# A gated recurrence inside a decoder step: token pairs up to 32 apart as 32x32 products in one PSUM tile

## The chip, the cores and the metric

The program runs on 1 core of one Trainium2 chip. The time is device microseconds from launch to end, one number for each execution; smaller is better.

## What is computed

One inference step of a two-layer decoder, for a prompt of 1024 tokens and 8 single-token samples with a paged cache of 8192 tokens each. Each layer has an input projection, four groups of heads (sparse attention, the HGRN2 recurrence, pooling, memory attention) and an output projection. The change is in the recurrence of the prompt. The reference runs it in chunks of tokens; with G the running sum of the log gates inside a chunk, it computes

```python
diff = Gc[:, :, :, None, :] - Gc[:, :, None, :, :]
dec = jnp.exp(jnp.where(causal[None, None, :, :, None], diff, -jnp.inf))
A = jnp.einsum('bhtd,bhtsd->bhts', qc, dec * kc[:, :, None, :, :])
o = jnp.einsum('bhts,bhsv->bhtv', A, vc) + jnp.einsum('bhtd,bhdv->bhtv', qc * jnp.exp(Gc), S)
```

There are 4 heads of 64 channels. A[t, s] is a sum over channels of q[t] exp(G[t] - G[s]) k[s] for s <= t. The decay depends on the channel and on both tokens, so A is no plain product of two matrices.

## The kernel before

Each layer runs through four phases, A, P2, P3 and O. A scheduler places the instructions of a phase on each engine's own queue, by priority and by modelled times, so that one stretch of work fills the gaps of another. The change lies in P3. There two stretches share the engines. `stageC` compresses the whole cache of the 8 samples: it gathers cache rows into `R` (SyncE, ScalarE and GpSimd issue the transfers), copies a part of them on VectorE (line 544), turns them on TensorE into `ct` (line 246), splits `ct` into a high and a low half (`Xh` on ScalarE at line 564, `Xl` on VectorE at line 565), and multiplies them by `w1h` and `w1l` into `ch` (lines 120 to 122). Its 16 units per layer have the lower priority. The other stretch, with the higher priority, is the sample set-up, the recurrence (`hgrn`), and after it the window and memory attention of the samples.

`hgrn_pair` takes two heads at a time, 64 channels each, on the 128 partitions, and 1024 tokens in four pieces of 256. For each piece `hgrn_blocks` is called once: 8 calls a layer, 16 in the program. A call works on two blocks `j` of 128 tokens and two heads `e`. To get A by matrix products it uses levels lv = 64, 32, 16, 8, 4, 2, 1. At a level the block is cut into groups of 2 lv tokens, and `decayed(lv)` makes a tile `hKQ` (VectorE subtracts, ScalarE takes exponents into `hE`, GpSimd multiplies) that holds in the first half of each group k times its decay to the middle of the group, and in the second half q times its own. The product of first halves with second halves gives the pairs that first part company at this level. The diagonal is k times q (line 1410).

- Levels 64, 32 and 16: TensorE writes each group's square straight to its place in a PSUM tile `bv` (line 1417), on top of the diagonal product; VectorE masks `bv` into the SBUF tile `hAT` (line 1421).
- Levels 8, 4, 2 and 1: TensorE multiplies each whole block of 128 tokens by itself (line 1429), and VectorE copies the pairs that belong to the level into `hAT` under a mask (line 1432), once for each head and level.

Then TensorE multiplies `hAT` by the values (line 1440), beside the product of `qG` with the state (line 1438), into one PSUM tile `O`. A product of float32 operands is two passes of a weight load and a matmul each, and the trace counts passes. In P3 the recurrence's lane has two PSUM tiles of kind `mt` and one of kind `ma` (`psT` and `psA`).

Of the kernel before, what the change touches and what calls it, by code (L numbers as in the profile page):

```python
# [9 lines left out]
F32 = mybir.dt.float32  # L10
# [4 lines left out]
U8 = mybir.dt.uint8  # L15
# [19 lines left out]
LEVELS = (8, 4, 2, 1)  # L35
# [5 lines left out]
def _const_array():  # L41
# [15 lines left out]
    put("causT", (i[:, None] <= i[None, :]))  # L57
# [22 lines left out]
    for lv in LEVELS:  # L80
        same = (i[:, None] // (2 * lv)) == (i[None, :] // (2 * lv))
        put(f"lev{lv}", same & (i[:, None] % (2 * lv) < lv) & (i[None, :] % (2 * lv) >= lv))
# [30 lines left out]
class Net:  # L113
# [52 lines left out]
    def setup(self, ctx):  # L166
# [8 lines left out]
        self.lev = {lv: self.cp.tile([128, 128], U8, name=f"levm{lv}") for lv in LEVELS}  # L175
# [23 lines left out]
    def late_setup(self, tp):  # L199
# [5 lines left out]
        for lv in LEVELS:  # L205
            nc.vector.tensor_copy(self.lev[lv], self.cc(tp, f"lev{lv}"))
# [1008 lines left out]
    def hgrn(self, l, pp, wk, nb=1):  # L1215
# [6 lines left out]
        for x in self.hst:  # L1222
            nc.gpsimd.memset(x, 0.0)
# [124 lines left out]
    def hgrn_blocks(self, l, hp, b, t0_, q, k, G, G3, EGl, hv, S0, gB, wk):  # L1348
# [39 lines left out]
        def decayed(lv):  # L1388

            E = t1("hE", 4)  # L1390
# [14 lines left out]
        cT = self.c("causT").unsqueeze(1).to_broadcast([128, 2, 128])  # L1405
        bv = [self.psA()[:, :256].rearrange("p (j t) -> p j t", j=2) for _ in range(2)]
        for e, hs in enumerate(half):
            for j in range(2):
                t0 = (b + j) * 128
# [9 lines left out]
        AT = [wk.tile([128, 2, 128], F32, name="hAT") for _ in range(2)]  # L1419
        for e in range(2):  # L1420
            nc.vector.tensor_tensor(AT[e], bv[e], cT, op=OP.mult)
        for g in range(2):
            ps = [self.psT() for _ in range(2)]
            for m in range(2):
                x = decayed(LEVELS[g * 2 + m])
                for e, hs in enumerate(half):
                    for j in range(2):
                        xj = x[hs, j * 128:j * 128 + 128]
                        mm(ps[e][:, m * 256 + j * 128:m * 256 + j * 128 + 128], xj, xj, start=True, stop=True)  # L1429
            for e in range(2):  # L1430
                for m in range(2):
# [369 lines left out]
```

## Time and profile before

| | |
|---|---|
| time before, median of 3 runs | 2343.73 us (2340.57 to 2345.09) |
| profiled execution | 2343.6 us, its span 2341.8 us |
| TensorE busy, of the span | 87% |
| VectorE busy | 65% |
| ScalarE busy | 38% |
| GpSimd busy | 32% |
| mean granted TensorE clock | 0.93 |
| recurrence in layer 0 and layer 1 | about 609 to 868 us and 1757 to 2061 us |

The busy shares are over the whole span. What a change in the recurrence is worth is read from the two stretches in which it runs.

### The profile page before, as it was taken

Reading aid. Unit: us, or ns where it says so; the run is one execution under the profiler, and the core shown is the slowest. Engines: PE = TensorE matmul, PEld = TensorE weight load, DVE = VectorE, ACT = ScalarE, POOL = GpSimd, SP = SyncE. Lnnn points to the kernel's source line nnn. Section 1 sums busy time; section 2 is a strip of 40 time slices with the busy share of each in tenths; the row PEclk is TensorE's granted clock in tenths of the full one; section 3 lists DMA queues with packets and bytes.
Section 4 is the critical chain, followed back from the end, with each engine's and each line's share of the span. In section 5 each row is a group of like instructions: output and inputs, shape, how many; then the busy total and the mean of one; then the engine's idle time right before and its main releaser. Section 6 shows DMA issues by size and latency. Waiting matters only on the chain.

```text
span 2341.8 us, 41952 instructions
## 1 busy us (share of the span) xinstructions
PE 2048.5 (87%) x14396; PEld 1824.7 (78%) x14396; DVE 1511.6 (65%) x3927; ACT 888.2 (38%) x2221; POOL 746.7 (32%) x841
## 2 busy tenths in 40 slices
PE   4999998894798999896979999898949899998878
PEld 4997888784788888785669979887838888878645
DVE  7874377885777666553298724788867776656523
ACT  4223366553433323230152234675545333333101
POOL 2002123313655543223020012243146555532340
PEclk8999999997899899898989999999969998998889
DMA  7237321106655446776253363221086544467661
GB/s 249 92 109 184 94 78 52 58 26 169 176 146 149 119 125 184 201 235 200 87 171 105 112 155 98 66 61 47 28 208 170 140 135 136 138 190 221 174 206 51
DMA packets 324093, 312.97 MB, mean 134 GB/s; under 512 B 60619, under 2 KB 285783, under 8 KB 323608
## 3 DMA queue, kind: packets, MB, share of 16 engines
q1 hardware_dynamic: 261544, 213.25, 31.1%
q0 software_dynamic: 24320, 79.71, 11.7%
q10 hardware_dynamic: 38016, 17.32, 2.8%
q8 instruction: 115, 1.88, 0.3%
q14 instruction: 98, 0.80, 0.1%
HBM read 255.00 MB, written 59.57 MB: 134 GB/s over the span
## 4 chain that ended last, share of the span: by engine, by line
PE 58%; DVE 16%; DMA 11%; issue 8%; ACT 3%; POOL 2%; SPq 2%; ACTq 0%; DVEq 0%; another core or an unknown queue 0%; POOLq 0%
PE ch L120 3%; PE ch L122 3%; PE mt L246 3%; PE ct L246 3%; PE ch L121 3%; PE aa L121 3%; PE aa L122 3%; PE aa L120 3%; PE mt L1429 2%; PE oa L122 2%; PE oa L120 2%; PE oa L121 2%; DVE P L804 2%; PE fa L120 2%; PE fa L122 2%
## 5 line engine op out<-in xcount | busy, mean ns | idle before, releaser
L524 POOL DMA_INDIRECT R<-in_cache_nsa_dram,idxc x256 | 253.1, 989 | 295.8 <-PE ct L246 192.5
L120 PE MATMUL ch<-w1h,Xh 128*128 128x256 f32 x1024 | 314.3, 307 | 17.6 <-ACT Xh L564 8.7
L122 PE MATMUL ch<-w1h,Xl 128*128 128x256 f32 x1024 | 311.4, 304 | 6.1 <-DVE Xl L565 3.2
L121 PE MATMUL ch<-w1l,Xh 128*128 128x256 f32 x1024 | 308.7, 301 | 0.4 <-issue 0.4
L120 PEld LDWEIGHTS ch<-w1h,Xh 128*128 128x128 f32 x1024 | 209.1, 204 | 23.5 <-ACT Xh L564 10.2
L122 PEld LDWEIGHTS ch<-w1h,Xl 128*128 128x128 f32 x1024 | 208.4, 204 | 13.8 <-DVE Xl L565 5.7
L148 POOL TENSOR_TENSOR wl<-wf,wh 128x1024 fp32r<-128x1024 f32 (+2 forms) x42 | 94.9, 2271 | 377.1 <-ACT wh L139 295.6
L564 ACT CAST Xh<-ct 128x512 fp32r<-128x512 f32 x256 | 146.0, 585 | 180.0 <-PE ct L246 109.9
L121 PEld LDWEIGHTS ch<-w1l,Xh 128*128 128x128 f32 x1024 | 209.0, 204 | 2.0 <-issue 0.4
L565 DVE TENSOR_TENSOR Xl<-ct,Xh 128x512 fp32r<-128x512 f32 x256 | 172.4, 683 | 42.8 <-ACT Xh L564 26.1
L246 PE MATMUL ct<-cst,R 128*128 128x128 f32 x1024 | 163.9, 292 | 40.7 <-DVE Xl L565 31.0
L246 PEld LDWEIGHTS ct<-cst,R 128*128 128x128 f32 x1024 | 122.1, 149 | 53.2 <-DVE Xl L565 33.7
L544 DVE COPY R<-R 128x256 f32<-128x256 f32 x260 | 92.5, 370 | 107.5 <-DMA R<-in_cache_nsa_dram,idxc 68.9
L121 PE MATMUL aa<-wl,hTh 128*128 128x326 f32 (+1 forms) x512 | 156.6, 307 | 5.1 <-POOL wl L148 5.1
L120 PE MATMUL aa<-wh,hTh 128*128 128x326 f32 (+1 forms) x512 | 156.4, 307 | 4.0 <-ACT wh L139 4.0
L122 PE MATMUL aa<-wh,hTl 128*128 128x326 f32 (+1 forms) x512 | 156.1, 305 | 0.0
L447 ACT ACTIVATE P<-ms,nst 128x512 f32<-128x512 f32 (+3 forms) x192 | 106.6, 557 | 78.7 <-DVE nst L777 78.0
L120 PE MATMUL fa<-hTh,wh 128*128 128x344 f32 x384 | 129.4, 337 | 4.2 <-ACT fo L381 3.9
L122 PE MATMUL fa<-hTh,wl 128*128 128x344 f32 x384 | 125.1, 326 | 0.0
L121 PE MATMUL fa<-hTl,wh 128*128 128x344 f32 x384 | 125.1, 326 | 0.0
L820 DVE TENSOR_TENSOR pl<-mt,ph 128x512 fp32r<-128x512 f32 (+1 forms) x160 | 101.2, 644 | 33.9 <-ACT ph L819 29.0
L777 DVE TENSOR_REDUCE nst<-ms 128x1 f32<-128x512 f32 (+3 forms) x192 | 98.0, 517 | 32.4 <-PE ms L774 19.2
(558 smaller groups left out, 5722.9 us busy)
## 6 DMA issues: line engine op xcount, KB each, us to landing
wf<-in_w_in_dram SPq DMA_DIRECT2D x34, 512.0 KB
R<-in_cache_nsa_dram SPq DMA_DIRECT2D x256, 64.0 KB
R<-in_cache_nsa_dram ACTq DMA_DIRECT2D x256, 64.0 KB
zd<-fo SPq DMA_DIRECT2D x48, 172.0 KB
pwf<-in_cmp_w_dram SPq DMA_DIRECT2D x32, 256.0 KB
wof<-in_w_out_dram SPq DMA_DIRECT2D x16, 512.0 KB
oo<-od SPq DMA_DIRECT2D x16, 512.0 KB
oz<-zd SPq DMA_DIRECT2D x16, 512.0 KB
```

What stands on the lines that cost most here:

```text
L120: mm(out, lh, rh, start=first, stop=False)
L121: mm(out, lh, rl, start=False, stop=False)
L122: mm(out, ll, rh, start=False, stop=last)
L148: e.tensor_tensor(lo, src, hi.bitcast(F32), op=OP.subtract)
L246: self.nc.tensor.transpose(out, in_, self.ident[:in_.shape[0], :in_.shape[0]])
L447: self.nc.scalar.activation(out, S, AF.Exp, bias=nm, accum_out=sm)
L524: nc.gpsimd.indirect_dma_start(R[:, j].rearrange("p c d -> p (c d)"), None, rows, bass.IndirectOffsetOnAxis(ap=self.idxc[:, l, at + j:at + ...
L544: nc.vector.tensor_copy(Rs[:, :, :, 2], R[:, :, 0:2])
L564: nc.scalar.copy(hi, pv)
L565: nc.vector.tensor_tensor(lo, pv, hi.bitcast(F32), op=OP.subtract)
L777: nc.vector.tensor_reduce(one(nm), S, axis=AX.X, op=OP.max, negate=True)
L820: nc.vector.tensor_tensor(pl[:, :n], ps[:, :n], ph[:, :n].bitcast(F32), op=OP.subtract)
```

## The change

All levels up to 16 become products of 32 tokens by 32 tokens. For each head, one PSUM tile holds for both blocks six products (k by q, and levels 16, 8, 4, 2, 1), each in 32 columns: the four groups of 32 tokens in a block stand on the four quarters of the partitions. VectorE multiplies the whole 128x384 tile by one mask (`near`: the diagonal, and one pattern for each level) into `hpn` and sums the six products into `hC`, 128x64. Levels 64 and 32 go to a PSUM tile `far`, and ScalarE copies their three pieces into a tile `hA` which was zeroed once (four such tiles take turns). `O` is now the product of `hA` with the values, plus four 32-row products of `hC` with the values. `causT`, the four level masks and their set-up go; `hE` has 3 buffers and not 4.

```diff
-LEVELS = (8, 4, 2, 1)
+LEVELS = (16, 8, 4, 2, 1)
...
-        for x in self.hst:
+        self.hat = [pp.tile([128, 2, 128], F32, name=f"hA{n}") for n in range(4)]
+        for x in self.hst + self.hat:
             nc.gpsimd.memset(x, 0.0)
...
-            E = t1("hE", 4)
+            E = t1("hE", 3)
             x = t1("hKQ", 5)
...
-                mm(bv[e][:, j], k[hs, t0:t0 + 128], q[hs, t0:t0 + 128], start=True, stop=True)
-        for lv in (64, 32, 16):
-            x = decayed(lv)
-            for e, hs in enumerate(half):
+        x64, x32 = decayed(64), decayed(32)
+        xs = [(k[:, sl], q[:, sl])] + [(x, x) for x in map(decayed, LEVELS)]
+        near = self.c("near").rearrange("p (m t) -> p m t", t=32).unsqueeze(1)
+        for e, hs in enumerate(half):
+            far = self.psA()[:, :192].rearrange("p (j t) -> p j t", j=2)
+            for j in range(2):
+                a0 = j * 128
+                mm(far[:, j, 0:64], x64[hs, a0:a0 + 128], x64[hs, a0 + 64:a0 + 128], start=True, stop=True)
+                for p in (0, 64):
+                    mm(far[p:p + 64, j, 64:96], x32[hs, a0 + p:a0 + p + 64], x32[hs, a0 + p + 32:a0 + p + 64],
+                       start=True, stop=True)
+            nc.scalar.copy(A[0:64, :, 64:128], far[0:64, :, 0:64])
+            for p in (0, 64):
+                nc.scalar.copy(A[p:p + 32, :, p + 32:p + 64], far[p:p + 32, :, 64:96])
...
+            ps = self.psT()[:, :2 * m * 32].rearrange("p (j m t) -> p j m t", j=2, m=m)
+            for n, (xk, xq) in enumerate(xs):
                 for j in range(2):
-                    for p in range(0, 128, 2 * lv):
-                        a0 = j * 128 + p
-                        mm(bv[e][p:p + lv, j, p + lv:p + 2 * lv], x[hs, a0:a0 + lv], x[hs, a0 + lv:a0 + 2 * lv],
-                           start=True, stop=True)
-            nc.vector.tensor_tensor(AT[e], bv[e], cT, op=OP.mult)
...
-                        mm(ps[e][:, m * 256 + j * 128:m * 256 + j * 128 + 128], xj, xj, start=True, stop=True)
-                    nc.vector.copy_predicated(AT[e], self.lev[LEVELS[g * 2 + m]].unsqueeze(1).to_broadcast([128, 2, 128]),
-                                              ps[e][:, m * 256:m * 256 + 256].rearrange("p (j t) -> p j t", j=2))
+                    for p in range(0, 128, 32):
+                        a0 = slice(j * 128 + p, j * 128 + p + 32)
+                        mm(ps[p:p + 32, j, n], xk[hs, a0], xq[hs, a0], start=True, stop=True)
+            nc.vector.tensor_tensor(pn, ps, near.to_broadcast([128, 2, m, 32]), op=OP.mult)
+            nc.vector.tensor_reduce(c, pn.rearrange("p j m t -> p j t m"), axis=AX.X, op=OP.add)
...
-                mm(O[:, j, e], AT[e][:, j], hv[:, b + j, e * 64:e * 64 + 64], start=S[j] is None, stop=S[j] is None or e == 1)
+                mm(O[:, j, e], AT[e][:, j], v, start=S[j] is None, stop=False)
+                for p in range(0, 128, 32):
+                    mm(O[ps, j, e], C[e][ps, j], v[ps], start=False, stop=S[j] is None or e == 1, tile_position=(p, p))
```

The scheduler works the order out anew for phases P3 and O; A and P2 keep theirs but for the mask set-up. On TensorE, in the second call of layer 0, the queue before holds the diagonal and the direct squares of one head (1410, 1417), then whole-block products (1429), between the cache's transposes `ct`; sizes are weights by moving columns, and x counts products of two passes each:

```order
L1410 MATMUL ma<-hq,hk 128x128 x2
L1417 MATMUL ma<-hKQ 64x64 x2
L1417 MATMUL ma<-hKQ 32x32 x4
L1417 MATMUL ma<-hKQ 16x16 x8
L606 MATMUL ch<-w_8493,hh 128x128
L246 MATMUL ct<-cst,R_9073 128x128
L609 MATMUL ch<-w_8493,hl 128x64
L246 MATMUL mt<-cst,ot 128x128 x2
L1429 MATMUL mt<-hKQ 128x128 x4
```

In the changed kernel, whose line numbers are its own, the same call has the far products (1414, 1416), then nearly all 96 near products (1430) in one go, and later the output (1440, 1443, 1446):

```order
L1414 MATMUL ma<-hKQ 128x64
L1416 MATMUL ma<-hKQ 64x32 x2
L1414 MATMUL ma<-hKQ 128x64
L1416 MATMUL ma<-hKQ 64x32 x2
L243 MATMUL mt<-cst,ot 128x128 x2
L1430 MATMUL mt<-hq,hk 32x32 x8
L1430 MATMUL mt<-hKQ 32x32 x24
L1440 MATMUL ma<-hS_6592,hqG 128x128
L1443 MATMUL ma<-hv,hA_6599 128x64
L1430 MATMUL mt<-hKQ 32x32 x8
L1430 MATMUL mt<-hq,hk 32x32 x8
L1430 MATMUL mt<-hKQ 32x32 x48
```

The short products stand closer together than any before, and the large ones are gone. Over a layer the last product of the recurrence stands behind 799 of the layer's 1696 `ch` products, where it stood behind 1036; in layer 1 it stands 192 `ch` products earlier.

On VectorE, at the third call of layer 0 before, eight masked copies of the call (1432, masks `levm`) lie between the cache's `Xl` (565) and `R` (544):

```order
L1432 COPY_PREDICATED hAT<-levm_64,mt 128x256
L1432 COPY_PREDICATED hAT<-levm_65,mt 128x256
L586 TENSOR_TENSOR xs<-ch,cbias 128x256
L565 TENSOR_TENSOR Xl_9523<-ct,Xh_9522 128x16x32
L544 COPY R_9665<-R_9665 128x2x2x64
L565 TENSOR_TENSOR Xl_9521<-ct,Xh_9520 128x16x32
L1432 COPY_PREDICATED hAT<-levm_64,mt 128x256
L544 COPY R_9649<-R_9649 128x4x64
L588 SCALAR_TENSOR_TENSOR xs<-xth,xs 128x256
L1432 COPY_PREDICATED hAT<-levm_66,mt 128x256
```

After, a call has two pairs of a product (1432) and a sum (1434) there:

```order
L1432 TENSOR_TENSOR hpn<-mt,cst 128x384
L562 TENSOR_TENSOR Xl_10123<-ct,Xh_10122 128x16x32
L1434 TENSOR_REDUCE hC<-hpn 128x64
L617 TENSOR_TENSOR vo<-ch,vo 128x64
L562 TENSOR_TENSOR Xl_10121<-ct,Xh_10120 128x16x32
L541 COPY R_10245<-R_10245 128x2x2x64
L541 COPY R_10229<-R_10229 128x4x64
L1432 TENSOR_TENSOR hpn<-mt,cst 128x384
L1434 TENSOR_REDUCE hC<-hpn 128x64
```

Ten VectorE instructions of a call, two maskings and eight copies, have become four.

## Rows read from the trace of the kernel before

**Rows 1.** The page, busy us of each engine, share of the span, instructions.

```profile
PE 2048.5 (87%) x14396; PEld 1824.7 (78%) x14396; DVE 1511.6 (65%) x3927; ACT 888.2 (38%) x2221; POOL 746.7 (32%) x841
```

**Rows 2.** Busy time by stretch: start:end, length, five engines, clock, DMA share, GB/s.

```profile
609.00:868.00 259.00, 236.90 (x2166) 216.05 (x2164) 183.89 (x499) 94.63 (x284) 143.92 (x213) 0.93 0.49 137
868.00:1000.00 132.00, 119.77 (x916) 108.07 (x915) 77.21 (x198) 40.57 (x91) 46.44 (x49) 0.95 0.64 181
1000.00:1060.00 60.00, 57.69 (x318) 48.74 (x316) 34.03 (x65) 16.29 (x28) 7.85 (x11) 0.94 0.81 240
1757.00:2061.00 304.00, 284.47 (x2535) 261.56 (x2535) 213.66 (x579) 114.39 (x318) 166.44 (x240) 0.93 0.53 146
```

**Rows 3.** TensorE's waits, 609 to 868 us: total us, times, longest.

```profile
PE ct L246 <- DVE Xl L565: 7.1, 4, 3.6
PE ct L246 <- DVE hE L1396: 3.1, 1, 3.1
PE ma L1410 <- DVE hS L1384: 2.5, 2, 1.9
PE ch L122 <- DVE Xl L565: 2.2, 2, 1.6
```

**Rows 4.** TensorE in order of time, layer 1: start us, us, instruction, passes.

```profile
1971.89 0.41 PE L1417 MATMUL ma<-hKQ 64*32 64x32 f32 x24
1972.23 1.16 PE L1429 MATMUL mt<-hKQ 64*128 64x128 f32 x8
1973.32 1.10 PE L246 MATMUL ct<-cst,R 128*128 128x128 f32 x8
```

**Rows 5.** The same view: one head's direct products, and a run of two passes.

```profile
631.53 0.71 PE L1410 MATMUL ma<-hq,hk 64*128 64x128 f32 x4
632.17 0.78 PE L1417 MATMUL ma<-hKQ 64*64 64x64 f32 x28
632.88 1.16 PE L1429 MATMUL mt<-hKQ 64*128 64x128 f32 x8
...
1897.07 0.21 PE L1417 MATMUL ma<-hKQ 64*16 64x16 f32 x2
1897.21 1.16 PE L1429 MATMUL mt<-hKQ 64*128 64x128 f32 x8
```

**Rows 6.** The same view: products with 64 moving columns, and what follows.

```profile
644.75 0.56 PE L1440 MATMUL ma<-hv,hAT 128*128 128x64 f32 x4
645.12 0.37 PE L121 MATMUL ch<-w1l,Xh 128*128 128x256 f32 x1
...
652.81 0.45 PE L1373 MATMUL ma<-hv,hkt 128*64 128x64 f32 x8
653.20 0.39 PE L120 MATMUL ch<-w1h,Xh 128*128 128x256 f32 x1
```

**Rows 7.** VectorE groups, 609 to 868 us: busy us, mean ns, idle before.

```profile
L565 DVE TENSOR_TENSOR Xl<-ct,Xh 128x512 fp32r<-128x512 f32 x71 | 47.9, 682 | 5.9 <-issue 2.9 <-ACT Xh L564 1.7 <-PE ct L246 0.6
L1432 DVE COPY_PREDICATED hAT<-levm,mt 128x256 f32<-128x256 uint8 x56 | 24.2, 443 | 14.2 <-PE mt L1429 13.7
L1421 DVE TENSOR_TENSOR hAT<-ma,cst 128x256 f32<-128x256 f32 x16 | 6.7, 421 | 17.4 <-PE ma L1417 10.7 <-PE ct L246 6.5
```

**Rows 8.** One tile's view: a sum on VectorE over 512 elements, min/median/max ns.

```profile
L1185 DVE TENSOR_REDUCE msST<-msK x16: 668/676/686, 948.3 to 2151.5; 128x8 f32<-128x512 f32 x16
```

**Rows 9.** ScalarE groups, 609 to 868 us: small copies out of PSUM.

```profile
L618 ACT COPY ko<-ch 64x128 f32<-64x128 f32 x8 | 2.1, 257 | 11.5 <-PE ch L606 11.3 <-issue 0.2
L619 ACT COPY vo<-ch 128x64 f32<-128x64 f32 x8 | 1.6, 203 | 0.0
```

**Rows 10.** Stretches of 5 us in the first call, columns as in rows 2.

```profile
615.00:620.00 5.00, 1.91 (x17) 1.71 (x16) 5.00 (x7) 1.86 (x6) 4.54 (x9) 1.00 0.52 110
620.00:625.00 5.00, 5.00 (x37) 4.38 (x36) 4.38 (x11) 2.37 (x8) 3.17 (x5) 0.66 0.78 209
...
630.00:635.00 5.00, 5.00 (x62) 4.49 (x63) 4.62 (x14) 1.97 (x7) 1.51 (x3) 1.00 0.20 54
```

More of the change, by code (lines that the diff above doesn't have):

```diff
@@ L56, in _const_array @@
     put("ident", np.eye(128))
-    put("causT", (i[:, None] <= i[None, :]))
+    r, c = i[:, None] % 32, np.arange(32)[None, :]
+    put("near", np.concatenate([r == c] + [(r // (2 * lv) == c // (2 * lv)) & (r % (2 * lv) < lv) & (c % (2 * lv) >= lv)
+                                           for lv in LEVELS], 1))
     t = 128 * np.arange(NT)[None, :] + i[:, None]
@@ L79, in _const_array @@
     put("sin", np.sin(ang).reshape(128, -1))
-    for lv in LEVELS:
-        same = (i[:, None] // (2 * lv)) == (i[None, :] // (2 * lv))
-        put(f"lev{lv}", same & (i[:, None] % (2 * lv) < lv) & (i[None, :] % (2 * lv) >= lv))
     put("mdiag", np.where(i[None, :] <= i[:, None], 0.0, NEG))
@@ L174, in setup @@
         self.mfar = self.cp.tile([128, 128], F32R, name="mfarr")
-        self.lev = {lv: self.cp.tile([128, 128], U8, name=f"levm{lv}") for lv in LEVELS}
         self.half = self.cp.tile([128, 1], F32, name="half")
@@ L1404, in hgrn_blocks @@
         half = (slice(0, 64), slice(64, 128))
-        cT = self.c("causT").unsqueeze(1).to_broadcast([128, 2, 128])
-        bv = [self.psA()[:, :256].rearrange("p (j t) -> p j t", j=2) for _ in range(2)]
+        x64, x32 = decayed(64), decayed(32)
+        xs = [(k[:, sl], q[:, sl])] + [(x, x) for x in map(decayed, LEVELS)]
+        near = self.c("near").rearrange("p (m t) -> p m t", t=32).unsqueeze(1)
+        m = len(xs)
+        AT, C = [], []
         for e, hs in enumerate(half):
+            far = self.psA()[:, :192].rearrange("p (j t) -> p j t", j=2)
@@ L1419, in hgrn_blocks @@
-        AT = [wk.tile([128, 2, 128], F32, name="hAT") for _ in range(2)]
-        for e in range(2):
-            nc.vector.tensor_tensor(AT[e], bv[e], cT, op=OP.mult)
[L1422 to L1428, printed above, removed]
-                        mm(ps[e][:, m * 256 + j * 128:m * 256 + j * 128 + 128], xj, xj, start=True, stop=True)
-            for e in range(2):
-                for m in range(2):
-                    nc.vector.copy_predicated(AT[e], self.lev[LEVELS[g * 2 + m]].unsqueeze(1).to_broadcast([128, 2, 128]),
-                                              ps[e][:, m * 256:m * 256 + 256].rearrange("p (j t) -> p j t", j=2))
+                a0 = j * 128
@@ new lines, in hgrn_blocks @@
+            AT.append(A)
+            ps = self.psT()[:, :2 * m * 32].rearrange("p (j m t) -> p j m t", j=2, m=m)
+            for n, (xk, xq) in enumerate(xs):
+                for j in range(2):
+                    for p in range(0, 128, 32):
+                        a0 = slice(j * 128 + p, j * 128 + p + 32)
+                        mm(ps[p:p + 32, j, n], xk[hs, a0], xq[hs, a0], start=True, stop=True)
+            pn = wk.tile([128, 2, m, 32], F32, name="hpn", bufs=1)
+            nc.vector.tensor_tensor(pn, ps, near.to_broadcast([128, 2, m, 32]), op=OP.mult)
@@ L1434, in hgrn_blocks @@
+            c = wk.tile([128, 2, 32], F32, name="hC", bufs=3)
+            nc.vector.tensor_reduce(c, pn.rearrange("p j m t -> p j t m"), axis=AX.X, op=OP.add)
+            C.append(c)
         ot = wk.tile([128, 2, 2, 64], F32, name="ot")
@@ L1439, in hgrn_blocks @@
             for e in range(2):
-                mm(O[:, j, e], AT[e][:, j], hv[:, b + j, e * 64:e * 64 + 64], start=S[j] is None, stop=S[j] is None or e == 1)
+                v = hv[:, b + j, e * 64:e * 64 + 64]
+                mm(O[:, j, e], AT[e][:, j], v, start=S[j] is None, stop=False)
+                for p in range(0, 128, 32):
+                    ps = slice(p, p + 32)
+                    mm(O[ps, j, e], C[e][ps, j], v[ps], start=False, stop=S[j] is None or e == 1, tile_position=(p, p))
         nc.scalar.copy(ot, O)
```

5 lines of the change are left out of this document (2 added, 3 removed).

## The prediction, made before the changed kernel ran

> **What bounds the kernel now.** I read the page first: TensorE is busy 87% of the span, VectorE 65% [rows 1]. That is an average, so I cut the span at the recurrence. In its two stretches, 259 and 304 us long, TensorE is busy 236.9 and 284.5 us, idle only 22.1 and 19.5 us [rows 2]. VectorE is busy 183.9 and 213.7 us there (71% and 70%), ScalarE 37% and 38%, GpSimd 56% and 55%, and the transfers move 137 and 146 GB/s where the program reaches 240 later [rows 2]. So TensorE sets the pace: it runs its queue in order, and the cache compression fills what the recurrence leaves. VectorE comes next, and the longest of TensorE's waits are for it: 7.1 + 2.2 us for the cache's low half `Xl`, 3.1 us for a level's subtraction `hE`, 2.5 us for the state [rows 3]. A microsecond of TensorE work saved in a call should therefore come out of the time almost whole; one saved on VectorE is worth a tenth of that or so; ScalarE and GpSimd have room.
>
> **TensorE, what goes.** I take start to start of neighbours, since a shown duration includes the pipeline. The diagonal of a head takes 631.53 to 632.17 = 0.64 us, and there are two in a call: 1.28 us [rows 5]. The direct squares take 632.17 to 632.88 = 0.71 us a head: 1.42 us [rows 5]. The whole-block products are 32 passes in four runs of 8, each 1972.23 to 1973.32 = 1.09 us: 4.36 us [rows 4]. The product of `hAT` with the values stays, as `hA`. In all 7.06 us a call go.
>
> **TensorE, what comes.** The near products are 96 products of 32 by 32, 192 passes. The nearest rows are the small squares. A run of 24 passes (8 with 32 columns, 16 with 16) takes 1971.89 to 1972.23 = 0.34 us [rows 4]; a run of 2 takes 0.14 us [rows 5]. So 22 more passes cost 0.20 us, 9 ns each, and some 0.12 us is the price of a run, the change of the array's shape. The 16-column passes lie on all four quarters of the partitions, as the new ones do; the 32-column ones lie on two. Upper bound: the mean of a whole run with its 64-column passes and its change, 0.71/28 = 25 ns [rows 5]. The new passes are twice as wide as most of the 24, so I take 11 ns: 192 x 11 = 2.1 us, and 0.4 us for some three runs a call, 2.5 us (bounds 2.0, and 192 x 25 = 4.9, which I keep as a rival; 3.3 at 15 ns ends the likely case).
>
> Here a rule speaks against the change. The Trainium skill (TensorE: Matmul & The Clock Gate, section Back-to-back issue gap) says that start to start never falls below about 25 ns however few the columns. The 9 ns of the small squares disagree with it, pass by pass. By the rule the near products would be 192 x 25 = 4.8 us, an estimate from that page, and the sum below that of the first rival.
>
> The far products are 8 passes of 128 weights by 64 columns and 16 of 64 by 32. The first are like the product of `hAT`: 4 passes in 644.75 to 645.12, 92 ns each [rows 6], 0.7 us; the second at 15 ns, 0.2 us; and the array changes shape eight times, 8 x 0.12 = 1.0 us: 1.9 us (1.4 with 49 ns for the first, as the 64-column passes at 652.81 [rows 6], and 0.1 a change; 2.1 with 25 ns for the second).
>
> The output gains 32 passes of 32 rows and 64 columns in four runs. No row has this shape. Below: the short passes' 15 ns; above: 49 ns, 8 passes in 652.81 to 653.20 with twice the weights [rows 6]. I take 25, 0.8 us, and eight changes, 1.0 us: 1.8 us (1.4 to 2.5). The Trainium skill (TensorEngine Tiling (Array Packing), section Gotcha 1: PSUM Pressure) says that tiles on different rows can't write one PSUM bank at the same time, and these four do; by it this term is at its upper end, and the sum below would be 0.7 us a call worse, 2337 us. No run so far shows it.
>
> Sum: 2.5 + 1.9 + 1.8 = 6.2 us come for 7.06 that go, 0.86 us a call, 16 calls: 13.8 us. These prices are at a granted clock of 1.00; the stretches have 0.93 [rows 2], so 15 us. Bounds of the likely case: 4.8 us come, 36 us gained; 7.9 come, 13 us lost.
>
> **VectorE.** Two maskings of 421 ns and eight copies of 443 ns go, 4.39 us [rows 7]. Two products over 384 elements come: between 421 ns at 256 and 682 ns at 512 elements [rows 7], 0.55 us. Two sums over 384 come: 676 ns at 512 [rows 8], 0.54 us at the slope of the products, although a stride of 32 elements is not in that row (bound: 0.68). So 2.2 us a call come, 2.2 go for good: 18 us a layer off 184 to 214. The 14.9 us of TensorE's waits for VectorE in the first stretch [rows 3] should shrink by that tenth, 3 us for both layers, and with them perhaps one fall of the clock (1.7 us, see the rivals): I put 4 us (0 to 10). Fewer buffers for `hE` work the other way: VectorE stands still until GpSimd has read the tile, with the cache's `Xl` behind it, which TensorE's transposes wait for. The 3.1 us wait is of that kind.
>
> **The rest.** ScalarE gets six copies a call, 257 ns and 203 ns for the like [rows 9]: 2 x (0.26 + 0.2 + 0.2) = 1.3 us, 21 us in all. It is busy 95 of 259 us [rows 2], so the cover is its idle time; without it `Xh` is late, then `Xl`, then the transposes, and the whole 21 us would show. The levels stay seven, so GpSimd and the exponents cost what they did; four zeroings more a layer lie ahead of the first call, where GpSimd waits for data. The constants grow by 64 columns of 636 in a transfer at the start, and four masks with their copies go: nothing either way.
>
> Against the profiled execution, 2343.6 us (the median of the runs is 2343.7): 2343.6 - 15 - 4 = 2325 us.
>
> **Rivals.**
> - Short passes at the mean of a mixed run (slower). If 192 passes in a row cost 25 ns, because 32 columns fill a quarter longer than 16 or because instructions come no faster, the near products are 4.9 us, 2.4 more; with 16 calls and the clock 41 us: 2343.6 - 19 + 41 = 2366 us. For it: no row has more than 24 such passes together. Against it: 9 ns in that row. It ends level at (15 + 4)/16/192, some 6 ns above my 11. The page's floor of 25 ns is this rival.
> - The clock falls (slower). In the first call TensorE is busy 1.9 of 5 us, and the next 5 us have a granted clock of 0.66 [rows 10], that is 2.4 GHz for a third and 1.2 GHz for two thirds: 3.4 us at half speed, 1.7 us lost. Short products leave most of the array unused; if the clock fell after each call's burst, 16 x 1.7 = 27 us, 2352 us. It decides at 11 falls. Against it: a run of 28 at 632.17 [rows 5] lies in 5 us with a granted clock of 1.00 [rows 10].
> - TensorE's time is not the limit (no change). The recurrence ends earlier in the queue, so more of the cache compression runs alone, as at 868 to 1000: 181 GB/s, TensorE 91% busy [rows 2]. If that part waits for its gathers, the 19 us turn into waits: 2343 us. For it: 12 us of TensorE's idle time there. Against it: 240 GB/s soon after.
> - VectorE matters more than its waits say (faster). If half of the 35 us saved on VectorE shows as shorter waits and fewer falls of the clock: 2343.6 - 15 - 18 = 2311 us, and 2302 with the near products at 9 ns.
>
> **How the numbers follow.** Forecast 0.58 (2325, own range 2305 to 2340: its bounds would need three terms at one end together), VectorE 0.11, no change 0.14, short passes 0.10, clock 0.07. A measurement here tells 0.2%, some 4.7 us, from no change. Faster: 0.58 + 0.11 = 0.69; same 0.14; slower 0.17. The range 2302 to 2353 leaves out the short-pass rival and half of the clock's, some 0.15, and a little below.
>
> **What would show it.** Right: runs of 1430 at 9 to 15 ns a pass, the far group near 1 us a head, TensorE's work in a call down by about a microsecond, VectorE's by 2.2, and the recurrence over some 10 us earlier or more of the cache done by its end. Wrong: 25 ns a pass; the output's 32-row passes above 49 ns; granted clocks below 0.9 in the two stretches; or waits for `R` in place of the time saved.

## The result and the profile after

The changed kernel took 2371.67 us (median of 6 runs, 2359.71 to 2379.11), the kernel before 2340.57 us beside it (6 runs, 2334.29 to 2345.09). The ratio is 1.0122, 95% interval 1.0090 to 1.0154: 1.2% slower, some 29 us, and outside the range that was given. The changed kernel's line numbers are three less than before's in most places.

The page of the changed kernel, busy time of each engine and the queue that carries instructions (packets, MB):

```profile
span 2369.8 us, 46829 instructions
PE 2048.4 (86%) x16828; PEld 1821.5 (77%) x16828; DVE 1505.1 (64%) x3827; ACT 907.1 (38%) x2317; POOL 737.9 (31%) x849
q8 instruction: 134, 2.20, 0.4%
```

TensorE is as busy as before [rows 1], 2048 us, in a span that is 28 us longer. Its passes went up by 2432 to 16828, and that queue, which had 115 packets and 1.88 MB, carries 134 and 2.20 MB.

The stretches of the recurrence in the changed kernel, which answer to [rows 2]:

```profile
608.00:860.00 252.00, 223.00 (x3251) 199.33 (x3252) 171.22 (x446) 95.52 (x315) 135.07 (x205) 0.90 0.46 127
1774.00:2058.00 284.00, 256.92 (x3485) 231.88 (x3485) 189.57 (x488) 110.70 (x338) 153.05 (x228) 0.89 0.49 135
```

TensorE's idle time is 29.0 and 27.1 us where it was 22.1 and 19.5, and the granted clock 0.90 and 0.89 where it was 0.93. The recurrence ends in fewer microseconds, and the compression behind it takes that back and more. So the whole compression stretch of a layer, from the first `Xl` to the last `vo`, is what to compare. Before, then after:

```profile
581.50:1037.30 455.80, 408.70 (x3387) 370.46 (x3388) 303.00 (x757) 161.92 (x414) 212.17 (x286) 0.92 0.58 165
1738.40:2197.60 459.20, 408.20 (x3380) 370.93 (x3380) 310.70 (x761) 168.81 (x420) 224.57 (x286) 0.90 0.58 164
```

```profile
578.50:1050.50 472.00, 407.46 (x4605) 367.69 (x4606) 302.44 (x709) 171.55 (x462) 212.76 (x290) 0.90 0.55 159
1755.20:2225.60 470.40, 412.85 (x4603) 371.78 (x4604) 301.58 (x715) 178.37 (x468) 215.64 (x290) 0.89 0.57 159
```

915 us became 942: nearly the whole loss lies here, 16 us of it in layer 0 and 11 in layer 1. To see its parts I cut these stretches into pieces of 1 us and multiplied TensorE's busy time in each by the clock granted in it: I call that its work in microseconds at 2.4 GHz, and the rest of the busy time what the clock cost. For both layers together:

| both layers, us | before | after | difference |
|---|---|---|---|
| TensorE work at full clock | 755.3 | 739.7 | -15.6 |
| lost to the lower clock | 61.5 | 80.6 | +19.1 |
| TensorE idle | 98.1 | 122.1 | +24.0 |

The work fell as forecast (13.8 us). It was given back one and a half times by idle time and once more by the clock. The split counts a little too much as clock: at a granted clock of 0.50, 80 of the near passes took 1.22 us (1974.98 to 1976.20 below), 15 ns each and not twice the 11 that they take at 1.00.

Where TensorE stood still, from its waits in layer 1's recurrence (total us, times, longest; before, see [rows 3] for layer 0):

```profile
PE mt L1430 <- issue: 16.2, 29, 2.1
PE ma L1414 <- DVE hS L1383: 2.8, 1, 2.8
PE ct L243 <- issue: 2.6, 2, 2.2
```

"issue" is a wait for nothing that the profile shows. With 4.5 us in layer 0 it is 20.7 us before the near products. This is how it looks in TensorE's order of time (start, us, instruction, passes, idle before it):

```profile
725.71 0.33 PE L1430 MATMUL mt<-hq,hk 64*32 64x32 f32 x16
725.86 0.88 PE L1430 MATMUL mt<-hKQ 64*32 64x32 f32 x80
726.95 0.33 PE L1430 MATMUL mt<-hq,hk 64*32 64x32 f32 x16 [0.22 <-ACT hoc L1465]
727.10 0.95 PE L1430 MATMUL mt<-hKQ 64*32 64x32 f32 x80
727.98 0.49 PE L1440 MATMUL ma<-hS,hqG 128*128 128x128 f32 x2
...
1970.60 0.33 PE L1430 MATMUL mt<-hq,hk 64*32 64x32 f32 x16
1970.75 1.04 PE L1430 MATMUL mt<-hKQ 64*32 64x32 f32 x53
1972.34 0.26 PE L1430 MATMUL mt<-hKQ 64*32 64x32 f32 x4 [0.55 <-issue]
1973.11 0.22 PE L1430 MATMUL mt<-hKQ 64*32 64x32 f32 x2 [0.51 <-issue]
1973.85 0.25 PE L1430 MATMUL mt<-hKQ 64*32 64x32 f32 x4 [0.52 <-issue]
1974.59 0.37 PE L1430 MATMUL mt<-hKQ 64*32 64x32 f32 x11 [0.49 <-issue]
...
1974.98 1.30 PE L1430 MATMUL mt<-hKQ 64*32 64x32 f32 x80
1976.20 0.79 PE L1440 MATMUL ma<-hS,hqG 128*128 128x128 f32 x2
```

The first call runs 16 passes in 0.15 us, 9.4 ns each, and 80 in 0.88 us, 11.0 ns each: the forecast's price to the nanosecond. In the second, after 69 passes, TensorE does two to four and then stands still for 0.5 us, again and again. What differs is the traffic (columns as in [rows 2]):

```profile
725.50:728.50 3.00, 2.78 (x200) 2.46 (x199) 2.45 (x5) 1.32 (x5) 0.84 (x2) 1.00 0.15 47
1970.00:1976.50 6.50, 4.34 (x200) 3.66 (x198) 3.12 (x7) 2.36 (x9) 3.35 (x5) 0.86 0.53 142
```

The changed kernel has five runs of 192 near passes with no other work between them. In this profile and that of e5 below I took the busy share of the DMA engines from 1 us ahead of each run to its end. The six with 50% or more all have three or four stalls of some 0.5 us. Of the four with at most 10%, two have no stall, and two have a single one, of 2.1 and 1.9 us, before their last four passes. So there are two kinds: short stalls where the traffic is dense, and long ones that come with little traffic too.

Then the clock falls (same columns):

```profile
1960.00:1972.00 12.00, 11.70 (x164) 10.73 (x164) 7.33 (x29) 5.71 (x23) 3.48 (x6) 1.00 0.08 21
1972.00:1975.00 3.00, 1.14 (x45) 0.85 (x48) 0.69 (x1) 1.09 (x4) 1.50 (x2) 0.95 0.72 189
1975.00:1977.00 2.00, 2.00 (x103) 1.94 (x91) 1.87 (x3) 0.00 (x0) 0.00 (x0) 0.50 0.66 191
1977.00:1982.00 5.00, 5.00 (x32) 4.65 (x31) 3.09 (x6) 1.18 (x3) 3.18 (x5) 0.55 0.55 144
1982.00:1985.00 3.00, 3.00 (x41) 2.46 (x42) 0.92 (x4) 0.85 (x2) 2.84 (x7) 1.00 0.63 185
```

TensorE is busy 1.1 of 3 us, and the next 7 us run at or near 0.50, that is 1.2 GHz, although it is busy all the time: 3.4 us lost. I count near passes less than 3 us apart as one burst. Bursts of 30 or more that began at full clock number 36 in the two profiles: 22 of the 23 with more than 0.45 us of stalls saw a fall from their start to 2 us behind their end, 5 of the 13 without. In all the clock falls 29 times in the two compression stretches, 15 times before.

VectorE's groups in the whole profile (busy us, mean ns, idle before):

```profile
L1395 DVE TENSOR_TENSOR hE<-hG 128x256 f32<-128x256 f32 x112 | 58.4, 535 | 33.1 <-POOL hKQ L1400 33.1
L1434 DVE TENSOR_REDUCE hC<-hpn 128x64 f32<-128x384 f32 x32 | 26.4, 825 | 0.6
L1432 DVE TENSOR_TENSOR hpn<-mt,cst 128x384 f32<-128x384 f32 x32 | 17.8, 556 | 24.7 <-PE mt L1430 18.7 <-remote 5.1
```

The product costs the 0.55 us that were forecast, the sum 0.82 us and not 0.54. VectorE stands still 33.1 us before `hE`, waiting for GpSimd's `hKQ`, where it was 5.4. TensorE's waits for `Xl` went from 40.6 to 60.8 us.

### The profile page after: what moved, and what is told of

It is laid out like the page before. It is cut to its first block, busy times and chain, and to the rows that moved or that the text cites. A ratio compares the mean times of both kernels' runs of the same rounds, so it can differ in the third digit from the quotient of the medians.

```text
span 2369.8 us, 46829 instructions
## 1 busy us (share of the span) xinstructions
PE 2048.4 (86%) x16828; PEld 1821.5 (77%) x16828; DVE 1505.1 (64%) x3827; ACT 907.1 (38%) x2317; POOL 737.9 (31%) x849
## 4 chain that ended last, share of the span: by engine, by line
PE 58%; DVE 15%; DMA 9%; issue 9%; ACT 3%; POOL 3%; SPq 1%; another core or an unknown queue 1%; ACTq 0%; DVEq 0%; POOLq 0%
PE ct L243 4%; PE ch L120 3%; PE mt L243 3%; PE ch L122 3%; PE ch L121 3%; PE oa L120 3%; PE oa L121 3%; PE aa L121 3%; PE aa L122 3%; PE aa L120 3%; PE oa L122 3%; DVE P L801 2%; DMA R<-in_cache_nsa_dram,idxc 2%; PE fa L120 2%; PE fa L121 2%
## 5 line engine op out<-in xcount | busy, mean ns | idle before, releaser
L120 PEld LDWEIGHTS ch<-w1h,Xh 128*128 128x128 f32 x1024 | 210.1, 205 | 16.9 <-DVE xs L583 9.1
L243 PE MATMUL ct<-cst,R 128*128 128x128 f32 x1024 | 174.2, 307 | 53.8 <-DVE Xl L562 45.7
L243 PEld LDWEIGHTS ct<-cst,R 128*128 128x128 f32 x1024 | 132.6, 159 | 64.3 <-DVE Xl L562 52.1
L541 DVE COPY R<-R 128x256 f32<-128x256 f32 x260 | 100.9, 406 | 124.8 <-DMA R<-in_cache_nsa_dram,idxc 82.5
```

Of the source, the lines that this page charges most:

```text
L120: mm(out, lh, rh, start=first, stop=False)
L243: self.nc.tensor.transpose(out, in_, self.ident[:in_.shape[0], :in_.shape[0]])
L541: nc.vector.tensor_copy(Rs[:, :, :, 2], R[:, :, 0:2])
```

## The experiments

Four theories were set against each other: (1) long runs of short passes starve TensorE of instructions, it stands still and its clock falls; (2) VectorE stands still for want of `hE` or `hKQ` buffers; (3) the new order of the queues alone; (4) a short pass costs its 11 ns and the loss comes from elsewhere. The runs were made in five groups. The kernel before took 2277, 2347, 2276, 2336 and 2339 us in them, so ratios to it are compared, and profiles within a group or between the two groups with 2277 and 2276 us. The scheduler works out the order of the queues anew for each edited kernel, so an edit of the passes changes that order too.

### e1: wide products in place of the near ones

```diff
-            for n, (xk, xq) in enumerate(xs):
+            for n, (xk, xq) in ((0, xs[2]), (3, xs[5])):
                 for j in range(2):
-                    for p in range(0, 128, 32):
-                        a0 = slice(j * 128 + p, j * 128 + p + 32)
-                        mm(ps[p:p + 32, j, n], xk[hs, a0], xq[hs, a0], start=True, stop=True)
+                    a0 = j * 128
+                    mm(ps[:, j, n:n + 3], xk[hs, a0:a0 + 128], xq[hs, a0:a0 + 96], start=True, stop=True)
```

> The changed kernel with the 48 near products of a head replaced by 4 products of 128 weights by 96 columns (8 passes for 96), into the same tile; it leaves out the pairs within 32 tokens, everything behind the products is as it was. Theory 1 (short passes: in the changed kernel TensorE takes 46 us for the near passes and stands still 20.7 us before them with nothing to wait for, in both layers together): about 20 us of wide passes take the place of 67, and the granted clock of the recurrence, 0.89 to 0.90, goes back to 0.93, so 2372 - 47 - 10 = 2315 us, below the kernel before. Theory 2 (VectorE stands still before its subtraction for want of hE buffers, and Xl is late): that stays, and only the 26 us of busy time go or less, 2345 us or more. Theory 3 (the new order of the queues alone): anything, with no stall before line 1430's products.

Measured: 2258.61 us beside 2276.92, ratio 0.9913 (0.9888 to 0.9938). The stalls are gone. Against e2, the kernel before with the same three buffers of `hE`, TensorE's work in the compression stretches is 20.5 us less, its idle time 3.6 us less, the clock's part 0.3 us more, and the stretches are 23.9 us shorter in the two profiles; the medians of the two times differ by 14 us. So here, with the rest of the new layout in place, most or all of the work saved came out of the time. A run of 8 wide passes takes 1.05 us, 34 us in all. So the near products, with all that they bring, cost the 2.1% between this ratio and 1.0122, some 48 us, and those 34: 82 us, 27 ns a pass, where they run at 9 to 11. Theory 4 falls, unless the order of the queues, which changed as well, is what brings the rest.

### e2 and e3: three or four buffers of hE

```diff
 (e2, the kernel before)
-            E = t1("hE", 4)
+            E = t1("hE", 3)
 (e3, the changed kernel)
-            E = t1("hE", 3)
+            E = t1("hE", 4)
...
-        self.hat = [pp.tile([128, 2, 128], F32, name=f"hA{n}") for n in range(4)]
+        self.hat = [pp.tile([128, 2, 128], F32, name=f"hA{n}") for n in range(3)]
```

> The kernel before with 3 buffers of hE for 4 and nothing else. Theory 1: within 5 us of before, 2335 to 2345. Theory 2: half of the loss or more is here, 2355 to 2370 us, with VectorE's idle time before hE up from 5 us to some 30 and the cache's transposes waiting for Xl about 30 us where it was 17 in the two layers. Theory 3: some 5 to 10 us to either side.

> The changed kernel with 4 buffers of hE, and 3 tiles hA for 4 to make the room. Theory 1: within 5 us of the changed kernel, 2365 to 2375. Theory 2: 2340 to 2355 us, VectorE's idle time before hE back to some 5 to 10 us. Theory 3: 5 to 10 us to either side.

Measured: e2 0.9982 (0.9956 to 1.0008), VectorE's idle time before `hE` 3.8 us; e3 1.0110 (1.0067 to 1.0153), 17.7 us. The fourth buffer is worth nothing in the one kernel or the other, to within half a per cent: theory 2 falls for the number of `hE` buffers. It hardly shortens VectorE's wait either, which is 23.4 us in e4 and 19.9 in e12 with three buffers and like times, so what that wait itself costs is not tested. In this group the stalls before line 1430 were 6.9 us, a third of the first profile's, and the loss was the same. That was the first sign that theory 1 is not all.

### e4: level by level

```diff
...
-            for n, (xk, xq) in enumerate(xs):
...
+        for n, (xk, xq) in enumerate(xs):
+            for e, hs in enumerate(half):
                 for j in range(2):
                     for p in range(0, 128, 32):
                         a0 = slice(j * 128 + p, j * 128 + p + 32)
-                        mm(ps[p:p + 32, j, n], xk[hs, a0], xq[hs, a0], start=True, stop=True)
+                        mm(pss[e][p:p + 32, j, n], xk[hs, a0], xq[hs, a0], start=True, stop=True)
...
```

> The changed kernel with the near products written level by level, both heads at a level, into two tiles at once, where they were written head by head: the same products, in runs of 32 passes as each hKQ comes, and an hKQ buffer is free after its level. Theory 1: if the stalls before line 1430's products come of long runs, 20.7 us falls to 5 and the time to about 2350; if of the number of passes, they stay. Theory 2: hKQ and hE come free earlier, VectorE's 33 us of idle time before hE fall to some 10, 2350 us too, but with the stalls still there. Theory 3: 5 to 10 us to either side.

Measured: 1.0106 (1.0066 to 1.0146), stalls 6.7 us, VectorE 23.4 us idle before `hE`. Inconclusive for the length of a run: the scheduler put the products of a call together again (seven runs of 192 passes, against five in the changed kernel).

### e5 to e7: half, all and twice the near passes

```diff
 (e6)
-            for n, (xk, xq) in enumerate(xs):
+            for n, (xk, xq) in enumerate(xs[:3]):
...
+            for j in range(2):
+                a0 = j * 128
+                mm(ps[:, j, 3:6], xs[5][0][hs, a0:a0 + 128], xs[5][1][hs, a0:a0 + 96], start=True, stop=True)
 (e7)
-                    for p in range(0, 128, 32):
+                    for p in list(range(0, 128, 32)) * 2:
```

> The changed kernel once more, beside the next three on one chip. Both theories: 1.2% slower than the kernel before. Theory 1 also expects TensorE's idle time of no visible cause before line 1430's products, 10 us or more in the two recurrence stretches together, and each fall of the granted clock there to follow one of those runs.

> The changed kernel with half of the near passes: the products of k with q and of levels 16 and 8 as they are, those of levels 4, 2 and 1 left out and their columns filled by two products of 128 by 96 a head (4 passes, some 0.45 us a head by the first experiment). The first experiment put the 3072 near passes at 48 + 26 = 74 us of time, 24 ns each, though they run at 9 to 11 ns. Theory 1 (instructions come too slowly for a long run, TensorE stands still, its clock falls): half of them cost 37 us or less, so 2372 - 74 + 37 + 13 = 2348 us on the first chip's scale, a ratio to before of 0.995 to 1.003. Theory 4 (a short pass costs its 11 ns and the rest comes from elsewhere): 17 + 13 for 34 us, ratio 1.008 to 1.012.

> The changed kernel with every near product made twice, into the same place, the same result: 3072 passes more. Theory 1: as dear as the first 3072, 74 us or more, since the instructions in store are used up sooner; ratio 1.040 to 1.050, with 40 us or more of idle time before line 1430's products and about as many falls of the clock as calls. Theory 4: 34 us and a few for the clock, ratio 1.027 to 1.030.

Measured: e5 1.0120 (1.0086 to 1.0154), e6 1.0046 (1.0021 to 1.0072), e7 1.0518 (1.0478 to 1.0558). The second 3072 passes cost 93 us, 30 ns each (26 to 34 by the two intervals). Half of the passes saved 17 us although 17 us of wide ones took their place: 22 ns each (16 to 29). From e5 to e7 the compression stretches show work +15, idle +33, clock +40 us; the waits before line 1430:

```profile
PE mt L1430 <- issue: 43.7, 31, 2.4
```

20.0 in e5, 14.6 in e6. A short pass costs 22 to 30 ns of time at every dose, and in e7 the smallest part of that is work.

Of e7's 31 waits, 22 last 1 us or more and make up 38.8 us. They too come with little traffic. In this run the DMA engines are 2% busy (837.5 to 843.8 us):

```profile
838.02 0.32 PE L1430 MATMUL mt<-hKQ 64*32 64x32 f32 x12
839.81 1.72 PE L1430 MATMUL mt<-hKQ 64*32 64x32 f32 x128 [1.47 <-issue]
843.81 1.38 PE L1430 MATMUL mt<-hKQ 64*32 64x32 f32 x84 [2.29 <-issue]
```

Between the two waits lie 128 passes. A pass is a weight load and a matmul, so that is 256 instructions, and a packet of the instruction queue carries about as many (19 packets more for 4877 instructions). One such packet starts at 841.4 us, and TensorE goes on 2.4 us behind it. Of the 22 long waits 21 begin within 2 us behind the start of a packet, where 28% of all near passes have one so close before them, and each of the 21 ends 2.2 to 3.0 us behind it. By these rows a long run of short passes does run out of instructions, as theory 1 has it. In the changed kernel itself only three waits (4.6 us) are that long.

### e9, e10, e13, e14 and e16 to e18: without the gathers

The gathers of cache rows are left out: tiles `R` are zeroed once a layer and used again, so the compression runs on zeros, and these runs are compared with one another. e9 and e16 are the kernel before, e10 and e17 the changed one, e13 and e18 that with e3's edit, e14 that with e3's and e4's.

```diff
-            R = xp.tile([128, 2, n, 64], F32, name=f"R{n}", tag=f"R{n}", bufs=rb if u is not None else 2)
...
+                ks = self.rfix[1].setdefault(n, [])
+                if len(ks) < rb:
+                    R = xp.tile([128, 2, n, 64], F32, name=f"R{n}", tag=f"R{n}", bufs=rb)
+                    nc.gpsimd.memset(R, 0.0)
+                    ks.append(R)
+                else:
+                    R = ks.pop(0)
+                    ks.append(R)
...
-                    nc.gpsimd.indirect_dma_start(R[:, j].rearrange("p c d -> p (c d)"), None, rows,
-                                                 bass.IndirectOffsetOnAxis(ap=self.idxc[:, l, at + j:at + j + 1], axis=0))
...
```

> The kernel before without the gathers of the cache rows: the tiles R are set to zero once a layer and used again and again, so that the compression works on zeros; TensorE's, VectorE's and ScalarE's work is as it was, GpSimd loses its gathers, and some 110 MB of 313 are not moved. It is the base for the next run; faster than before under every theory, by the waits for R and whatever the engines gain: 2270 to 2330 us on the scale of 2345.

> The changed kernel without those gathers. In the two profiles of the changed kernel every run of 180 near passes or more that lies in a stretch with DMA engines under 25% busy has no stall (5 runs), and every one with more has one (11 runs). Theory 1b (TensorE's instructions come late because they share the transfers with the gathers): no stalls of more than 3 us in all before line 1430's products here, falls of the clock as many as without the change, and this kernel 5 to 20 us faster than the kernel before without gathers, since the work on TensorE is 15 us less. Theory 1c (the length of the run alone uses up the instructions): the stalls stay near 20 us, and this kernel is 15 to 30 us slower than that one, as with gathers.

> The changed kernel without gathers and with 4 buffers of hE (3 tiles hA for 4). Without gathers the stalls before line 1430's products were gone, and still the changed kernel was some 20 us slower than the kernel before without gathers; VectorE stood still 49 us before hE there, 9 in the other, and TensorE was idle 23 us of its recurrence stretches where the other was 6. Theory 2b (the missing hE buffer, of use once the stalls are gone): VectorE's idle time before hE falls to 25 us or less and the ratio from 0.962 to 0.954 or below. Theory 5 (the buffers of hKQ, which are held until both heads' products are done, or the longer chain from far products to output): 45 us and 0.960 or above.

> As the run above, and the near products level by level for both heads, so that an hKQ buffer is free after its level. Theory 2b: like the run above. Theory 5 with hKQ: VectorE's idle time before hE falls below 25 us only here, ratio 0.955 or below. If both stay at 0.960 or above, the loss without stalls is not a matter of these buffers: then it is the clock (42 us lost in the two compression stretches without gathers after the change, 20 before) and the waits of the longer chain.

> The kernel before without gathers again, beside the next two on one machine. All theories: 0.953 to 0.957.

> The changed kernel without gathers again. If the loss of 0.85% against the kernel before without gathers holds here: 0.960 to 0.965. If it was chance: 0.956 or below.

> The changed kernel without gathers, with 4 buffers of hE. Theory 2b (the hE buffer is the second part of the loss): 0.957 or below and 0.5% or more below the run above. Theory 5: within 0.3% of the run above.

Measured: e9 0.9538 (0.9513 to 0.9564) and e10 0.9623 (0.9566 to 0.9680); in another group e13 0.9556 (0.9531 to 0.9582) and e14 0.9727 (0.9700 to 0.9755); and side by side e16 0.9401 (0.9369 to 0.9433, 2201.94 us), e17 0.9539 (0.9507 to 0.9571, 2234.01), e18 0.9525 (0.9493 to 0.9557, 2231.88).

Two things follow. The short stalls go with the gathers: of those below 1 us there are 32 before line 1430's products (1426 here) in the first profile, none in e10 and e17, one each in e13 and e18, with the same 3072 passes. The long ones do not need the gathers: e13 and e18 have two each and e14 has five, so that its stalls come to 10.4 us (4.6 in e13, 5.3 in e18). The counts in e10's expectation leave out the two long stalls that came with little traffic. And the loss does not need any stall: e17 is 32 us slower than e16 with none. Layer 1's recurrence in e16 and e17:

```profile
1700.00:1924.00 224.00, 220.19 (x2173) 203.16 (x2171) 175.79 (x507) 87.15 (x256) 70.91 (x129) 0.99 0.12 30
```

```profile
1705.00:1923.00 218.00, 201.07 (x3110) 181.38 (x3108) 156.74 (x430) 86.07 (x286) 70.99 (x133) 0.91 0.12 31
```

TensorE was idle 3.8 us and is idle 16.9, and the clock goes from 0.99 to 0.91. Its waits there are of many kinds, none large:

```profile
PE ma L1368 <- DMA hv<-hvd: 4.7, 1, 4.7
PE ct L244 <- DVE Xl L558: 4.4, 5, 1.7
PE ma L1442 <- DVE hC L1430: 3.8, 2, 2.7
PE ch L120 <- DVE xs L579: 1.2, 1, 1.2
PE mt L244 <- POOL hD L1359: 1.2, 2, 1.0
```

e18 equals e17, so the number of `hE` buffers is not the cause. e14 was to free `hKQ` sooner, but as in e4 the scheduler put the products together again (nine runs of 180 passes or more, four in e13); it is 40 us slower than e13 and does not settle the point. All of them leave VectorE 39 to 48 us idle before `hE`, where e16 has 10.

### e8, e11 and e15: hKQ in bf16

The operands of all levels are rounded to bf16, and a product is one pass where it was two. e8 is the changed kernel, e11 the kernel before, e15 is e8 with 7 buffers of `hKQ` and 4 of `hE`.

```diff
-            x = t1("hKQ", 5)
+            x = wk.tile([128, N], mybir.dt.bfloat16, name="hKQ", bufs=5)
```

> The changed kernel with hKQ in bf16 (it rounds the operands of all levels): the products of the six levels and the far ones are one pass of a load and a matmul where they were two, 112 near passes a call for 192 and 12 far ones for 24. Theory 1: as many products, but 40% fewer instructions, so stalls and falls of the clock go down by half or more, some 25 us less than the changed kernel, ratio 0.998 to 1.003. Theory 4: 80 x 16 passes of 11 ns and the far ones, 14 + 8 us, and no change in stalls, ratio 1.003 to 1.007.

> The kernel before with hKQ in bf16 and nothing else, to see what of the 1.1% gained by the changed kernel with bf16 is due to the change. The whole-block products (71 us in both layers) and the direct squares (25 us) become one pass for two, of 128 columns that need no more than half the time: 48 us or more of TensorE's work go, ratio 0.970 to 0.985, so better than the changed kernel with bf16 (0.989) if the short passes are what holds that one back; 0.995 or above if the change of layout is what gained there.

> The changed kernel with hKQ in bf16, and the room that this frees used for 7 buffers of hKQ (5 before) and 4 of hE (3 before). With 5 and 3 the ratio was 0.989. Theory 1: the stalls with gathers bind, and more buffers change nothing: 0.987 to 0.991. Theory 2b or 5: VectorE waits less and TensorE's waits for Xl fall by some 10 us, 0.983 to 0.987.

Measured: e8 0.9890 (0.9858 to 0.9922), faster than both kernels; e11 1.0009 (0.9990 to 1.0028); e15 0.9935 (0.9910 to 0.9961), so the buffers add nothing. From e5 to e8 the work falls by 36 us, the clock's part by 19, the idle time by 2; the stalls stay, 20.8 us. e11 is the surprise. Its TensorE work is 64 us below that of e2 (in its group the kernel before took 2276 us) and its compression stretches are 57 us shorter, and hardly any of it reaches the end: the time between the two stretches is 25 us longer than in e2 and the time behind the second 28. There TensorE waits for work that the scheduler had put there, in layer 0 from 985 to 1080 us, and has a granted clock of 0.82:

```profile
PE ma L1207 <- POOL msV L1205: 10.2, 1, 10.2
PE oa L120 <- DVE ox L1620: 6.9, 1, 6.9
```

So theory 3 seems to have a part: the order decides whether time saved in the recurrence is time saved.

### e12: the sum along neighbours

```diff
-            pn = wk.tile([128, 2, m, 32], F32, name="hpn", bufs=1)
-            nc.vector.tensor_tensor(pn, ps, near.to_broadcast([128, 2, m, 32]), op=OP.mult)
+            pn = wk.tile([128, 2, 32, m], F32, name="hpn", bufs=1)
+            nc.vector.tensor_tensor(pn.rearrange("p j t m -> p j m t"), ps, near.to_broadcast([128, 2, m, 32]), op=OP.mult)
...
-            nc.vector.tensor_reduce(c, pn.rearrange("p j m t -> p j t m"), axis=AX.X, op=OP.add)
+            nc.vector.tensor_reduce(c, pn, axis=AX.X, op=OP.add)
```

> The changed kernel with the masked product written so that the six products of a pair lie side by side, and the sum reads them in a row (it read with a stride of 32 elements, 821 ns for 384 elements; the product took 557). If the stride is what made the sum dearer than its 0.54 us, it falls to 540 to 680 ns and the product rises by less; 32 sums, 5 to 9 us of VectorE, worth 0 to 5 us of time: ratio 1.009 to 1.013. If a sum costs that anyhow, 821 ns stays.

Measured: 1.0122 (1.0094 to 1.0150). One tile's view (min/median/max ns) shows that the price of the stride only moved, from a read at every 32nd element to a write at every 6th:

```profile
L1432 DVE TENSOR_TENSOR hpn<-mt,cst x32: 830/856/900, 628.6 to 1991.1; 128x384 f32<-128x384 f32 x32
L1434 DVE TENSOR_REDUCE hC<-hpn x32: 532/553/587, 630.2 to 1992.0; 128x64 f32<-128x384 f32 x32
```

The sum got 0.27 us shorter, the product 0.30 us longer. Stalls were 5.1 us here, and the loss again the same.

## Why the prediction was wrong

**TensorE's work: right.** Removed, per call, by start to start in the two layers: diagonal, direct squares and whole blocks 7.3 and 7.5 us (7.06 at full clock forecast). Added: near products 2.65 and 3.1 without the stalls (2.5), far products 2.4 and 2.55 (1.9; a head takes 1.19 us, since the two 64-column passes of a block alone need 0.36), output 1.4 and 1.6 (1.8; 8 passes of 32 rows run in 0.24 us, below the 0.32 that the forecast's two prices give). At full clock the work is 15.6 us less, 13.8 forecast. That the 11 ns a pass came true is in part luck: the forecast had scaled it up from one row of narrower passes.

**The step that failed** is the price of the near products in the sum: "192 x 11 = 2.1 us, and 0.4 us for some three runs a call, 2.5 us". The passes did run at that price, but the sum put the idle time and the falls of the clock that come with them at nothing, on the strength of the first paragraph: "A microsecond of TensorE work saved in a call should therefore come out of the time almost whole". Four pairs of profiles show what that left out; the fifth has the new layout with wide products, the sixth the old layout in bf16 (compression stretches of both layers, us):

| pair | work | clock | idle | together |
|---|---|---|---|---|
| before to after | -15.6 | +19.1 | +24.0 | +27 |
| e2 to e12 (3 buffers of `hE` in both) | -10.5 | +23.8 | +17.1 | +30 |
| e9 to e10, no gathers | -10.7 | +21.7 | +20.7 | +32 |
| e16 to e17, no gathers | -10.3 | +20.8 | +26.7 | +37 |
| e2 to e1, wide products | -20.5 | +0.3 | -3.6 | -24 |
| e2 to e11, old layout, bf16 | -64.0 | +0.7 | +6.9 | -57 |

In the last two rows saved work does shorten the stretches almost whole, so the sentence on TensorE's work holds there. With the 3072 short passes, idle time and clock cost 41 to 48 us each time. That is the term that the sum lacked: all in, a near pass costs 22 to 30 ns and not 11. The whole spans of the first four pairs differ by 28, 20, 26 and 32 us, so from the second on part of it is regained outside the stretches.

The idle time has one thing in common in the four pairs: TensorE's waits for VectorE in these stretches grow by 14, 14, 18 and 21 us, and from e2 to e1 by 1. With the gathers, most of the rest is waits without a visible cause.

**The rivals.** Each had a piece. *The clock falls* had the size (27 us; 19 to 24 measured) but a chance of 0.07, weighed by one run of 28 passes, and tied the falls to the bursts as such. A burst alone seldom brings one (in e10, without stalls, 4 of 19 bursts at full clock); one with idle time in it nearly always does (22 of 23). *Short passes at 25 ns* had the price, for another reason: they run at 9 to 11 ns, as the forecast took from one row, and cost 22 to 30 in the end. The Trainium skill's page Runtime: NRT & Kernel Launch, section Instruction fetch mechanics, says that an engine streams its instructions in blocks by a DMA queue of its own and that this is mostly hidden. The rows agree with the queue and the blocks (19 packets more for 4877 instructions, 128 passes between two waits of e7) and not with the hiding (21 of e7's 22 long waits). What the short stalls of 0.5 us wait for, no row names. *TensorE's time is not the limit* was near: the 15 us did turn into waits, though for VectorE and not for gathers, and the clock made a loss of it.

**VectorE: the wrong sign.** Its relief is 4.39 - 2 x (0.557 + 0.821) = 1.6 us a call, 2.2 forecast; the sum over a stride lay beyond its bound. TensorE's waits for `Xl` grew. The sentence on fewer `hE` buffers foresaw VectorE's idle time (33 us before `hE`) but not its reason: a fourth buffer leaves 17.7 us in e3 and 42.7 in e18, and the time as it was.

**ScalarE: right.** Its busy time rose by 19 us, 21 forecast, and TensorE's waits for it did not grow.

**What stays open.** Why TensorE is idle 20 to 27 us more where there is no stall. What the profiles show fits a denser recurrence. Between its first and last pass in a layer lie 922 and 934 `ch` passes of the cache before, 791 and 807 in e1, 703 and 767 after, 503 and 555 in e7, and in the same order VectorE's idle time before `hE` rises: 5.4, 12.5, 33.1 and 53.8 us. Without gathers TensorE's share of busy time in layer 1's recurrence falls from 98 to 92% (e16, e17). So `Xl`, which stands behind `hE` in VectorE's queue, may come late because the scheduler packs the recurrence more tightly. No run held the order of the queues fixed, so it stays a guess how much of the price of a short pass is this order. Nor is it shown that any run freed `hKQ` sooner with float32 operands.

## What to carry to other kernels

Price a stream of very short passes by what it costs with everything around it (here 22 to 30 ns), not by its start to start: doubling or removing the passes measures that in one run. With TensorE some 90% busy, work saved came out whole here where the products stayed large (e1), and not where they became many short ones: there it bought idle time, and the idle time a lower clock for the work behind it. A version with fewer instructions for the same products (here one pass for two) gained 1.1%, while the same edit on the old layout gained nothing, its time being lost again behind the stretches.

## What the hardware showed unasked

- Passes of 32 by 32 tiles on four quarters of the array run 9.4 to 11.0 ns apart, in runs of 16 to 80.
- TensorE can stand still for 0.5 us after every two to four of such passes while gathers keep the DMA engines busy: 32 such waits in the first profile, none in e10 and e17.
- In e7 TensorE stood still 22 times for 1.0 to 2.4 us among such passes, with the DMA engines as little as 2% busy, and 21 times went on 2.2 to 3.0 us behind the start of a packet on the instruction queue.
- The same kernel took 2276 us in some groups of runs and 2336 to 2347 in others. In the latter TensorE waits without a visible cause at many places (16.9 us before line 948 in the first profile of the kernel before), in the former hardly (1.6 us before the line that has most of it in e2). The short stalls go the same way: 32 in the first profile and in e5, 1 to 7 in e3, e4 and e12, with the same loss.
- A stride costs VectorE some 0.3 us for 384 elements, whether the sum reads at every 32nd element or the product writes at every 6th.
